# Attention stage of a hybrid block: GpSimd in written order, the reciprocals' read on its queue, the second head's loads up front, later loads by plan, both table loads ordered

## The chip, the cores and the metric

The kernel runs on one core of a Trainium2 chip. The metric is the device time of one launch in microseconds (us), the median of several runs. Before the change the runs took 1646.33, 1641.17 and 1647.93 us.

A core has five engines with a queue each: PE (TensorE, matmuls), DVE (VectorE), ACT (ScalarE), POOL (GpSimd) and SP (SyncE, here only for DMAs). Each works through its own instructions in order and waits on semaphores for the others. DMAs are issued by SP, ACT and POOL and run beside the engines.

## The reference, cut to what matters

One layer for 1024 tokens of width 1024: a modulated norm, a projection, two mixers side by side (causal attention with forget gates and an RWKV-7 recurrence), gates, an output projection and a convolutional feed-forward part. The change touches the attention:

```python
def fox_attention(q, k, v, log_f):
    seq = q.shape[2]
    cum = jnp.cumsum(log_f, axis=-1)
    scale = FOX_HEAD_DIM ** -0.5
    outs = []
    for blk in range(seq // Q_BLOCK):
        q0 = blk * Q_BLOCK
        q1 = q0 + Q_BLOCK
        logits = jnp.einsum('bhqd,bhkd->bhqk', q[:, :, q0:q1], k[:, :, :q1]).astype(jnp.float32) * scale
        logits = logits + cum[:, :, q0:q1, None] - cum[:, :, None, :q1]
        causal = jnp.arange(q1)[None, :] <= (q0 + jnp.arange(Q_BLOCK))[:, None]
        logits = jnp.where(causal, logits, -jnp.inf)
        probs = jax.nn.softmax(logits, axis=-1).astype(v.dtype)
        outs.append(jnp.einsum('bhqk,bhkd->bhqd', probs, v[:, :, :q1]))
    return jnp.concatenate(outs, axis=2)
```

There are 8 heads of width 64, and `Q_BLOCK` is 128. The gates, `jax.nn.sigmoid(p_gate)`, are computed in the same stage of the kernel.

## The kernel before

**Stages.** Projections and the recurrence come first, then attention, then the gated merge and the feed-forward part. Numbers are kept as pairs of a rounded high part and a low rest (`hi`/`lo`, `th`/`tl`), so that each product takes several matmuls.

**A head.** Queries and keys of head `h` lie in DRAM (`d_st`), as four pieces; values lie in `d_v`. `load_head(h)` (L1093) issues three DMAs on POOL: `stA` (two pieces, 1 MB), `stB` (two pieces of 68 rows, 544 KB) and `vh` (values, 512 KB). Each tag has two buffers, so the load of head `h + 2` needs the end of head `h`. Head 0 has tiles of its own (`first`).

**A block.** Each head takes four blocks `I` of 256 query rows, in the order 3, 0, 2, 1, and head 7 in the order 0, 1, 3, 2. `s_chain` issues the logits `lg`: for 512 columns one matmul with `stA` and one with `stB`. `softmax` (L1148) adds the mask and takes the maximum on DVE, then exponentiates on ACT with the row sums beside it (`P`). `t_chain` transposes `P` on PE (`tp`), `halve` splits it on ACT and DVE, and `a_chain` multiplies it with the values (`ov`). `collect` (L1271) copies `ov` into the tile `o` on ACT and adds its other half on DVE. There is one tile `o` for two heads and half of the rows: `o01` belongs to heads 0 and 1 and the second half of the rows, `o00` to the first half, `o11` and `o10` to heads 2 and 3. There are two buffers for these tiles, so `o10` reuses the one of `o00`.

**The reciprocals.** The softmax's division is made at the end. When the sums of half a head are there, `spread` (L1194) copies their reciprocals from PSUM into `rt`, writes them to DRAM (`d_rs`) and reads them back, broadcast over 64 partitions, as `R`. Both DMAs are issued by ACT. After the second head of a pair, POOL multiplies `o` by `R` (two halves, L1290), casts the result to `fx[0]` (L1293) and subtracts for the rest `fx[1]` (two halves, L1296). These five instructions are called a group here. The end of a group frees the buffer of its `o`.

**What sets the order.** PE's order is written out everywhere. In the attention stage that of DVE and ACT is too. A planner (`Weave`) keeps a clock of its own; the chains say when they want to go on, and between their steps it fills PE with matmuls for the gates (`rk_ps`, turned into gates by ACT at L1325 and L1328). POOL's order is left to the scheduler of the framework, which moved the loads up as far as it could: the load of `stA3`, written in head 2's second block, is issued when its buffer comes free.

**ACT's tables.** ACT loads a table for exp and tanh with `preload_act_table_set("exp_and_others")` (L1340). Nothing ties that instruction to others, and it stands at the program's start, where the next load replaces it. In attention the load is put in again ahead of the first gate (L1325).

Of the kernel before, what the change touches and what calls it, by code (L numbers as in the profile page):

```python
# [9 lines left out]
F32 = mybir.dt.float32  # L10
F32R = mybir.dt.float32r
# [5 lines left out]
S = 1024  # L17
KT = 8
NH = 512
# [11 lines left out]
for _name, _k in (("c", 8), ("ln1_g", 8), ("b_mod", 48), ("ln2_g", 8), ("mu", 14), ("w0", 4), ("a0", 4),  # L31
                  ("k_k", 4), ("k_a", 4), ("r_k", 4), ("ln_w", 4), ("ln_b", 4), ("conv_b", 22), ("conv_w", 66)):
    VEC[_name] = (_n, _k)
    _n += _k
NVEC = _n
NOSYNC = mybir.DependencyInfo(mybir.DependencyClass.NoSync, mybir.DependencyReason.DATA)

CST = {}
# [97 lines left out]
def hybrid_block(ctx: ExitStack, tc: tile.TileContext, a, out):  # L136
# [63 lines left out]
    sig_c = nc.scalar.activation(sc, V("c", 0, 8), AF.Sigmoid)  # L200
    nc.vector.tensor_tensor(sc, sc, V("c", 0, 8), op=ALU.mult)

    def use_ln_exp(after=None):

        i = nc.scalar.preload_act_table_set("natural_log_exp_and_others")
        if after is not None:
            tc.add_manual_dep(i.ins, after.ins.name, NOSYNC)


    d_gate = dr.tile([16, 128, S], F32, name="d_gate")  # L210
# [125 lines left out]
    def gate_steps(w, i, pps, ptag, pool, tag):  # L336
        if weave.late == 1:
            yield from late_gate(w, i)
            return
        for hf in range(2):  # L340
            cs = slice(hf * NH, hf * NH + NH)
            ps = pps.tile([128, NH], F32, tag=ptag, name=f"gt{i}_{hf}")
            yield from gemm_steps(ps, w[0:2], u, cs)

            g = pool.tile([128, NH], F32, tag=tag, name=f"gs{i}_{hf}")
            if weave.late:
                nc.scalar.activation(g, ps, AF.Tanh, scale=0.5)
# [6 lines left out]
            stt(g, ps, 0.0, g, op0=ALU.min, op1=ALU.subtract)  # L354
            nc.scalar.activation(g, g, AF.Exp)
            nc.sync.dma_start(d_gate[i, :, cs], g)


# [1 line left out]
    with ExitStack() as es:  # L360
# [563 lines left out]
        def main(k, p, hf):  # L924
# [97 lines left out]
            nc.scalar.activation(rs, rs, AF.Exp, scale=-0.5)  # L1022
# [60 lines left out]
    heads = {}  # L1083

    def load_first():

        parts = [d_st[0, 0], d_st[0, 1], d_st[0, 2, 0:68, :], d_st[0, 3, 0:68, :], d_v[0].rearrange("p a x -> p (a x)")]
        tiles = [fxp.tile([128, S], F32R, tag=f"h{t}", name=f"first{t}") for t in (3, 7, 2, 6, 5)]
        for t, x in zip(tiles, parts):
            marks["head"] = nc.gpsimd.dma_start(t[0 : x.shape[0], :], x)  # L1090
        heads[0] = *tiles[0:4], tiles[4].rearrange("p (a x) -> p a x", x=128)

    def load_head(h):  # L1093
        A = at.tile([128, 2, S], F32R, tag="stA", name=f"stA{h}")
        nc.gpsimd.dma_start(A, d_st[h, 0:2, :, :].rearrange("k r s -> r k s"))
        B = at.tile([128, 2, S], F32R, tag="stB", name=f"stB{h}")
        nc.gpsimd.dma_start(B[0:68, :, :], d_st[h, 2:4, 0:68, :].rearrange("k r s -> r k s"))
        vh = at.tile([128, 8, 128], F32R, tag="vh", name=f"vh{h}")
        nc.gpsimd.dma_start(vh, d_v[h])
        heads[h] = A[:, 0, :], A[:, 1, :], B[:, 0, :], B[:, 1, :], vh  # L1100

    load_first()
    while len(weave.queue) > 12:
        weave.step()
    fx = [[fxp.tile([128, S], F32R, tag=f"h{4 * x + p}", name=f"fx{x}{p}") for p in range(4)] for x in range(2)]
    weave.finish()
    weave.late = 1

    with tc.manual_schedule(engines={mybir.EngineType.DVE, mybir.EngineType.Activation}):
# [12 lines left out]
        def s_chain():  # L1122

            yield 3500
            for k, (h, I) in enumerate(seq):
                if k % 4 == 1 and h < 7:
                    load_head(h + 1)
                qa, ka, qb, kb, _ = heads[h]
                for i in (2 * I, 2 * I + 1):
                    n = (i + 1) * 128  # L1130
                    qs = slice(i * 128, i * 128 + 128)
                    yield from slot(pl_free if i > 3 else ps_free)
                    if i > 3 or i % 2 == 0:
                        yield from slot(lg_free)
                        lgt = pl.tile([128, S], F32, tag="lg", name=f"lg{h}_{i}")

                    lg = lgt[:, i % 2 * NH :] if i < 4 else lgt
                    for c0 in range(0, n, NH):
                        c1 = min(n, c0 + NH)
                        mm(lg[:, c0:c1], qa[:, qs], ka[:, c0:c1], start=True, stop=False)  # L1140
                        mm(lg[:, c0:c1], qb[0:68, qs], kb[0:68, c0:c1], start=False, stop=True)
                    if i > 3:
                        weave.spawn(softmax(h, (i,), lgt), 351)
                    elif i % 2:
                        weave.spawn(softmax(h, (i - 1, i), lgt), 351)
                    yield 0

        def softmax(h, rows, lgt):  # L1148
# [15 lines left out]
                part.append((i, n, nm, lg))  # L1164
            yield t + 140 - weave.now
            for i, n, nm, lg in part:
                e = (at.tile([128, S], F32, tag="P", name=f"P{h}_{i}", bufs=4) if i > 3 else
                     at.tile([128, NH], F32, tag="Ps", name=f"P{h}_{i}", bufs=2))
                if (h, hf) not in sums:
                    sums[h, hf] = at.tile([128, 8], F32, tag="sums", name=f"sums{h}_{hf}", bufs=4), []  # L1170
                sm, done = sums[h, hf]
                total = nm[:, 1:2] if h == 7 else sm[:, i % 4 : i % 4 + 1]
                nc.scalar.activation(e[:, 0:n], lg[:, 0:n], AF.Exp, bias=nm[:, 0:1], accum_out=total)
# [19 lines left out]

        def spread(h, hf, tp):  # L1194
            p = h // 2
            rt = at.tile([4, 128], F32, tag="rt", name=f"rt{h}_{hf}", bufs=1)
            nc.scalar.copy(rt, tp[0:4, 384:512])
            t = weave.use("ACT", weave.now, 260)
            yield t + 300 - weave.now
            nc.scalar.dma_start(d_rs[h, hf * NH : hf * NH + NH].rearrange("(i k) -> i k", k=128), rt)  # L1200
            if h % 2 == 0:
                norms[p, hf] = at.tile([128, NH], F32, tag="R", name=f"R{p}{hf}", bufs=2)
            yield t + 3500 - weave.now
            nc.scalar.dma_start(norms[p, hf][h % 2 * 64 : h % 2 * 64 + 64, :],
                                d_rs[h : h + 1, hf * NH : hf * NH + NH].to_broadcast([64, NH]))
            landed.add((h, hf))

# [28 lines left out]
        def halve(h, I, jj, tp, w, last):  # L1236
# [11 lines left out]
            tp_free.append(t + 210)  # L1248
            av_queue.append((t + 210, h, I, jj, th, tl))

        def a_chain():

            for _ in range(8 * 10):
# [3 lines left out]
                yield t - weave.now  # L1257
                if jj == 0:
                    yield from slot(ov_free)
                vh = heads[h][4]  # L1260
                order = [(0, th), (1, th), (1, tl), (0, tl)] if jj == I else [(0, th), (0, tl), (1, th), (1, tl)]
                for x, (k, t) in enumerate(order):
                    o0 = 128 if (jj == I and k == 1) else 0
                    mm(ov_ps[:, o0:256], vh[:, 2 * jj + k, :], t[:, 256 * k : 256 * k + 256 - o0],
                       start=jj == 0 and x == 0, stop=jj == I and x == 3)
                th_free.append(weave.now + 260)
                if jj == I:
                    weave.spawn(collect(h, I), 260)
                yield 0

        def collect(h, I):  # L1271
            p, hf, oc = h // 2, I // 2, slice(I % 2 * 256, I % 2 * 256 + 256)
            rows = slice(h % 2 * 64, h % 2 * 64 + 64)
            if (p, hf) not in halves:
                halves[p, hf] = at.tile([128, NH], F32, tag="o", name=f"o{p}{hf}"), []
            o, got = halves[p, hf]
            nc.scalar.copy(o[rows, oc], ov_ps[rows, :])
            yield weave.use("ACT", weave.now, 270) + 140 - weave.now
# [58 lines left out]
            while pending or (weave.cur is begun and begun is not None):  # L1337
                yield 300

        nc.scalar.preload_act_table_set("exp_and_others")  # L1340
        weave.run([a_chain(), t_chain(), s_chain()])
        weave.late = 2
        weave.run([drain()])
# [25 lines left out]
    def br_open(x, n):  # L1369
        if (x, n) not in br_raw:  # L1370
            br_load(x, n)
        raw = br_raw[x, n]
        hi = br.tile([128, NH], F32R, tag="whi", name=f"hi_br{x}{n}")
        lo = br.tile([128, NH], F32R, tag="wlo", name=f"lo_br{x}{n}")
        nc.scalar.copy(hi, raw)
# [764 lines left out]
```

## Time and profile before

| What | Value |
|---|---|
| median of 3 runs | 1646.33 us |
| the profiled execution, time | 1646.9 us |
| the profiled execution, span on the core | 1645.1 us |
| mean granted clock of PE | 0.991 |
| DMA, mean over the span | 147 GB/s |
| stA, stB and vh loads on POOL's queue | 7 each |
| writes of reciprocals and reads of R on ACT's queue | 14 each |

The span runs from the first to the last instruction of the program on the core; the time of the execution is a little longer. Busy time of PE counts matmuls whose ends are modelled. "Idle before" an instruction, in square brackets, is followed by what ended it, as inferred from semaphores. In rows of POOL and of the queues, buffer numbers are left out of the names: `stA` can be any head's.

### The profile page before, as it was taken

Reading aid. Unit: us, or ns where it says so; the run is one execution under the profiler, and the core shown is the slowest. Engines: PE = TensorE matmul, PEld = TensorE weight load, DVE = VectorE, ACT = ScalarE, POOL = GpSimd, SP = SyncE. Lnnn points to the kernel's source line nnn. Section 1 sums busy time; section 2 is a strip of 40 time slices with the busy share of each in tenths; the row PEclk is TensorE's granted clock in tenths of the full one; section 3 lists DMA queues with packets and bytes.
Section 4 is the critical chain, followed back from the end, with each engine's and each line's share of the span. In section 5 each row is a group of like instructions: output and inputs, shape, how many; then the busy total and the mean of one; then the engine's idle time right before and its main releaser. Section 6 shows DMA issues by size and latency. Waiting matters only on the chain.

```text
span 1645.1 us, 25963 instructions
## 1 busy us (share of the span) xinstructions
PE 1614.0 (98%) x9756; PEld 1327.9 (81%) x9756; DVE 1197.2 (73%) x2334; ACT 808.4 (49%) x1473; POOL 139.7 (8%) x169
## 2 busy tenths in 40 slices
PE   7999999999999999999999999999999999999998
PEld 5777877887887778788888888888888888888886
DVE  6875887887876636777579346887777777786677
ACT  7663434443455546676524135644444444555455
POOL 0011101211111020222132000000000000000000
PEclk8999999999999999999999999999999999999999
DMA  9587644543343236543487310242332232675363
GB/s 346 185 314 228 166 129 122 136 121 91 111 119 89 89 107 179 135 136 106 148 322 259 135 65 27 83 135 96 104 114 96 96 109 97 223 256 160 122 211 109
DMA packets 123902, 241.72 MB, mean 147 GB/s; under 512 B 39816, under 2 KB 48320, under 8 KB 123776
## 3 DMA queue, kind: packets, MB, share of 16 engines
q1 hardware_dynamic: 114944, 220.94, 41.3%
q0 software_dynamic: 7600, 17.25, 3.8%
q10 hardware_dynamic: 1232, 1.86, 0.4%
q8 instruction: 77, 1.26, 0.3%
q14 instruction: 49, 0.40, 0.1%
HBM read 174.43 MB, written 65.56 MB: 146 GB/s over the span
## 4 chain that ended last, share of the span: by engine, by line
PE 88%; DVE 6%; ACT 3%; DMA 1%; issue 1%; POOL 0%; SPq 0%; DVEq 0%; ACTq 0%; POOLq 0%
PE X L144 14%; PE D L144 13%; PE Y L144 6%; PE gt L144 6%; PE ps_rkv L144 6%; PE wo L144 5%; PE br L144 5%; PE rk_ps L144 4%; PE qk L144 4%; PE W L144 3%; PE v L144 3%; PE ov L144 2%; PE lg L144 2%; PE tp L151 2%; PE low L144 1%; PE sp L144 1%
## 5 line engine op out<-in xcount | busy, mean ns | idle before, releaser
L144 PE MATMUL D<-op,op 128*128 128x512 f32 x924 | 209.8, 389 | 0.0
L144 PEld LDWEIGHTS D<-op,op 128*128 128x128 f32 x924 | 173.3, 188 | 36.3 <-DVE op L1403 0.3
L144 PE MATMUL X<-T_m,S 128*128 128x512 f32 x440 | 107.3, 390 | 0.1
L144 PEld LDWEIGHTS X<-T_m,S 128*128 128x128 f32 x440 | 82.4, 188 | 18.2 <-ACT T_m L1828 0.6
L1402 ACT CAST op<-g 128x512 fp32r<-128x512 f32 x77 | 47.8, 621 | 73.0 <-PE D L144 48.1
L1403 DVE TENSOR_TENSOR op<-g,op 128x512 fp32r<-128x512 f32 x77 | 53.0, 688 | 41.3 <-ACT op L1402 41.3
L1639 DVE SCALAR_TENSOR_TENSOR c<-ab,vec,c 128x512 f32<-128x512 f32 x88 | 65.9, 749 | 19.5 <-ACT c L1642 17.9
L1603 DVE TENSOR_TENSOR S<-ur,S 128x512 fp32r<-128x512 f32 x66 | 45.5, 691 | 35.6 <-ACT S L1599 35.5
L1246 DVE TENSOR_TENSOR tl<-tp,th 128x512 fp32r<-128x512 f32 (+1 forms) x80 | 49.9, 633 | 28.0 <-ACT th L1238 24.5
L270 DVE TENSOR_TENSOR lo_in<-raw_in,hi_in 128x512 fp32r<-128x512 f32 x84 | 57.9, 728 | 15.9 <-PE gt L144 7.7
L1599 ACT CAST S<-ur 128x512 fp32r<-128x512 f32 x66 | 41.0, 622 | 55.6 <-DVE ur L1592 30.6
L1603 DVE TENSOR_TENSOR A<-ur,A 128x512 fp32r<-128x512 f32 x64 | 44.0, 688 | 30.9 <-ACT A L1599 30.7
L266 ACT CAST hi_in<-raw_in 128x1024 fp32r<-128x1024 f32 x42 | 43.9, 1048 | 45.2 <-PE ps_rkv L144 28.0
L144 PE MATMUL Y<-T_h,A 128*128 128x512 f32 x264 | 63.5, 389 | 0.0
L795 DVE TENSOR_TENSOR t<-E,M 128x60 f32<-128x60 f32 (+24 forms) x248 | 54.8, 221 | 11.8 <-DMA M<-sm 5.7
L144 PE MATMUL Y<-T_h,S 128*128 128x512 f32 x264 | 63.3, 389 | 0.0
L799 DVE TENSOR_TENSOR E<-E,t 128x60 f32<-128x60 f32 (+24 forms) x248 | 57.9, 234 | 5.8
L144 PE MATMUL X<-B_b,A 128*128 128x512 f32 x252 | 60.8, 390 | 0.0
L144 PE MATMUL W<-B_f,A 128*128 128x512 f32 x252 | 60.6, 389 | 0.0
L1238 ACT CAST th<-tp 128x512 fp32r<-128x512 f32 (+1 forms) x80 | 42.4, 542 | 33.7 <-PE tp L151 31.3
L144 PEld LDWEIGHTS Y<-T_h,A 128*128 128x128 f32 x264 | 49.5, 188 | 10.4
L144 PEld LDWEIGHTS Y<-T_h,S 128*128 128x128 f32 x264 | 49.5, 188 | 10.3
(494 smaller groups left out, 4071.6 us busy)
## 6 DMA issues: line engine op xcount, KB each, us to landing
raw_in<-in_w_in SPq DMA_DIRECT2D x50, 512.0 KB
wm<-in_w_mod SPq DMA_DIRECT2D x48, 512.0 KB
ur<-in_w_up SPq DMA_DIRECT2D x44, 512.0 KB
g<-d_g SPq DMA_DIRECT2D x35, 512.0 KB
d_g<-gs SPq DMA_DIRECT2D x44, 256.0 KB
d_g<-c SPq DMA_DIRECT2D x33, 256.0 KB
d_st<-qh SPq DMA_DIRECT2D x64, 128.0 KB
d_gate<-gs SPq DMA_DIRECT2D x32, 256.0 KB
```

The lines of the kernel that those rows point to most:

```text
L144: weave.last = nc.tensor.matmul(o, lhsT, rhs, start=start, stop=stop, skip_group_check=more)
L266: i = nc.scalar.copy(hi, raw)
L270: nc.vector.tensor_tensor(lo[:, c : c + NH], raw[:, c : c + NH], f32(hi[:, c : c + NH]), op=ALU.subtract)
L795: i = tt(tv, E32[:, 0:J, s : s + 1].to_broadcast([128, J, W]), M32[:, s : s + 1, s + 1 : 32].to_broadcast([128, J, W]), op=ALU.mult)
L799: tt(E32[:, 0:J, s + 1 : 32], E32[:, 0:J, s + 1 : 32], tv, op=ALU.add)
L1238: nc.scalar.copy(th[:, 0:w], tp[:, 0:w])
L1246: tt(tl[:, 0:w], tp[:, 0:w], f32(th[:, 0:w]), op=ALU.subtract)
L1402: nc.scalar.copy(hi, src)
L1403: tt(lo, src, f32(hi), op=ALU.subtract)
L1599: nc.scalar.copy(hi, src)
L1603: tt(lo, src, f32(hi), op=ALU.subtract)
L1639: stt(c, ab[:, x + hf * NH : x + hf * NH + NH], V("conv_w", 22 * x + i), c, op0=ALU.mult, op1=ALU.add)
```

## The change

- POOL's instructions stand in written order in the attention stage, as those of DVE and ACT do.
- The read of `R` is issued by POOL instead of ACT. `rt` has two buffers.
- Queries and keys of head 1 are loaded ahead of the stage. Those of heads 2 to 7 are issued at the second block of the head before, and each waits for the matmul that was last in the program there. Values are loaded on their own: for heads 1 and 2 at the third and fifth block, for later ones after the last `ov` of head `h`.
- `o` has three buffers. The four large `P` tiles of a head have the width that their rows need, one buffer for each.
- Both loads of ACT's tables name the activations that they come after: the last ones that need the table before.

```diff
+SYNC = mybir.DependencyInfo(mybir.DependencyClass.Sync, mybir.DependencyReason.DATA)
...
-    def use_ln_exp(after=None):
+    def use_ln_exp(*after):
         i = nc.scalar.preload_act_table_set("natural_log_exp_and_others")
-        if after is not None:
-            tc.add_manual_dep(i.ins, after.ins.name, NOSYNC)
+        for x in after:
+            tc.add_manual_dep(i.ins, x.ins.name, NOSYNC)
...
+    def fetch(dst, src):
+        i = nc.gpsimd.dma_start(dst, src)
+        tc.add_manual_dep(i.ins, weave.last.ins.name, SYNC)
+
+    def load_v(h):
+        values[h] = at.tile([128, 8, 128], F32R, tag="vh", name=f"vh{h}")
+        nc.gpsimd.dma_start(values[h], d_v[h])
+
+    def load_head(h, fetch):
         A = at.tile([128, 2, S], F32R, tag="stA", name=f"stA{h}")
-        nc.gpsimd.dma_start(A, d_st[h, 0:2, :, :].rearrange("k r s -> r k s"))
+        fetch(A, d_st[h, 0:2, :, :].rearrange("k r s -> r k s"))
         B = at.tile([128, 2, S], F32R, tag="stB", name=f"stB{h}")
-        nc.gpsimd.dma_start(B[0:68, :, :], d_st[h, 2:4, 0:68, :].rearrange("k r s -> r k s"))
-        vh = at.tile([128, 8, 128], F32R, tag="vh", name=f"vh{h}")
-        nc.gpsimd.dma_start(vh, d_v[h])
-        heads[h] = A[:, 0, :], A[:, 1, :], B[:, 0, :], B[:, 1, :], vh
+        fetch(B[0:68, :, :], d_st[h, 2:4, 0:68, :].rearrange("k r s -> r k s"))
+        heads[h] = A[:, 0, :], A[:, 1, :], B[:, 0, :], B[:, 1, :]
     load_first()
+    load_head(1, nc.gpsimd.dma_start)
...
-    with tc.manual_schedule(engines={mybir.EngineType.DVE, mybir.EngineType.Activation}):
+    with tc.manual_schedule(engines={mybir.EngineType.Pool, mybir.EngineType.DVE, mybir.EngineType.Activation}):
...
-                if k % 4 == 1 and h < 7:
-                    load_head(h + 1)
+                if k % 4 == 1 and 0 < h < 7:
+                    load_head(h + 1, fetch)
+                if k in (2, 4):
+                    load_v(k // 2)
...
-                e = (at.tile([128, S], F32, tag="P", name=f"P{h}_{i}", bufs=4) if i > 3 else
+                e = (at.tile([128, n], F32, tag=f"P{i}", name=f"P{h}_{i}", bufs=1) if i > 3 else
...
-            rt = at.tile([4, 128], F32, tag="rt", name=f"rt{h}_{hf}", bufs=1)
+            rt = at.tile([4, 128], F32, tag="rt", name=f"rt{h}_{hf}", bufs=2)
...
-            nc.scalar.dma_start(norms[p, hf][h % 2 * 64 : h % 2 * 64 + 64, :],
+            nc.gpsimd.dma_start(norms[p, hf][h % 2 * 64 : h % 2 * 64 + 64, :],
...
+                ends[h] = ends.get(h, 0) + 1
+                if ends[h] == 10 and 0 < h < 6:
+                    load_v(h + 2)
...
-                halves[p, hf] = at.tile([128, NH], F32, tag="o", name=f"o{p}{hf}"), []
+                halves[p, hf] = at.tile([128, NH], F32, tag="o", name=f"o{p}{hf}", bufs=3), []
...
-        nc.scalar.preload_act_table_set("exp_and_others")
+        table = nc.scalar.preload_act_table_set("exp_and_others")
+        for x in ("early", "rs"):
+            tc.add_manual_dep(table.ins, marks[x].ins.name, NOSYNC)
...
-    use_ln_exp(marks["gate"])
+    use_ln_exp(marks["gate"], marks["hi"])
```

The order of PE's and DVE's instructions does not change. On POOL, before, from the loads of head 3 to those of head 4 (a name's last digits are a running number; `R01_7206` is filled by two reads, one for each head of a pair, and `x2` is two equal rows):

```order
L1095 DMA stA3_7452<-d_st_95 128x2x1024
L1097 DMA stB3_7454<-d_st_95 68x2x1024
L1290 TENSOR_TENSOR o01_7118<-o01_7118,R01_7206 128x256 x2
L1099 DMA vh3_7456<-d_v_96 128x1024
L1293 CAST fx00_6889<-o01_7118 128x512
L1296 TENSOR_TENSOR fx10_6893<-o01_7118,fx00_6889 128x256 x2
L1290 TENSOR_TENSOR o00_7160<-o00_7160,R00_7277 128x256 x2
L1293 CAST fx00_6889<-o00_7160 128x512
L1095 DMA stA4_7726<-d_st_95 128x2x1024
L1097 DMA stB4_7728<-d_st_95 68x2x1024
L1296 TENSOR_TENSOR fx10_6893<-o00_7160,fx00_6889 128x256 x2
```

The same stretch of POOL in the changed kernel:

```order
L1096 DMA stA3_7452<-d_st_95 128x2x1024
L1096 DMA stB3_7454<-d_st_95 68x2x1024
L1215 DMA R01_7206<-d_rs_97 64x512
L1306 TENSOR_TENSOR o01_7118<-o01_7118,R01_7206 128x256 x2
L1309 CAST fx00_6893<-o01_7118 128x512
L1312 TENSOR_TENSOR fx10_6897<-o01_7118,fx00_6893 128x256 x2
L1101 DMA vh3_7547<-d_v_96 128x1024
L1215 DMA R00_7277<-d_rs_97 64x512
L1306 TENSOR_TENSOR o00_7162<-o00_7162,R00_7277 128x256 x2
L1309 CAST fx00_6893<-o00_7162 128x512
L1312 TENSOR_TENSOR fx10_6897<-o00_7162,fx00_6893 128x256 x2
L1096 DMA stA4_7726<-d_st_95 128x2x1024
```

The two reads of R have come in, each behind a load, and the loads of head 4 now stand behind both groups instead of inside the second one. The same stretch comes again for the loads of heads 5 and 6, with `o11`, `vh5` and `o10`.

ACT before, from the last gate ahead of attention to the first one inside it (`gs` are gates, `hi_in36` the high part of a gate's weights, `P0_6` the first probabilities):

```order
L277 CAST hi_in36_6929<-raw_in36_6927 128x1024
L351 ACTIVATE gs8_1_6915<-gt8_1_6842 128x512
L352 ACTIVATE gs8_1_6915<-gs8_1_6915 128x512
L353 ACTIVATE gs8_1_6915<-gs8_1_6915 128x512
L355 ACTIVATE gs8_1_6915<-gs8_1_6915 128x512
L1173 ACTIVATE P0_6_6979,sums0_1_6980<-lg0_6_6948,nm0_6_6960 128x896
L1325 ACT_TABLE_LOAD
L1325 ACTIVATE gs9_0_6982<-rk_ps_6925 128x512
```

ACT in the changed kernel, behind the same gate:

```order
L356 ACTIVATE gs8_1_6919<-gs8_1_6919 128x512
L1356 ACT_TABLE_LOAD
L278 CAST hi_in36_6933<-raw_in36_6931 128x1024
L1184 ACTIVATE P0_6_6977,sums0_1_6978<-lg0_6_6952,nm0_6_6964 128x896
L1341 ACTIVATE gs9_0_6980<-rk_ps_6929 128x512
```

The table load has moved from behind the first probabilities to behind the last older gate, and the cast of the weights now follows it. The load at the program's start is gone.

More of the change, by code (lines that the diff above doesn't have):

```diff
@@ L354, in gate_steps @@
             stt(g, ps, 0.0, g, op0=ALU.min, op1=ALU.subtract)
-            nc.scalar.activation(g, g, AF.Exp)
+            marks["early"] = nc.scalar.activation(g, g, AF.Exp)
             nc.sync.dma_start(d_gate[i, :, cs], g)
@@ L1021, in main @@
             nc.scalar.activation(rs, va, AF.Ln, scale=1.0 / CH, bias=epsr[:, 1:2])
-            nc.scalar.activation(rs, rs, AF.Exp, scale=-0.5)
+            marks["rs"] = nc.scalar.activation(rs, rs, AF.Exp, scale=-0.5)
             stt(y, y, V("ln_w", p), rs, op0=ALU.mult, op1=ALU.mult)
@@ L1082, in hybrid_block @@
     pt = es.enter_context(tc.tile_pool(name="pt", bufs=2, space=PS))
-    heads = {}
+    heads, values = {}, {}
     def load_first():
@@ L1090, in load_first @@
             marks["head"] = nc.gpsimd.dma_start(t[0 : x.shape[0], :], x)
-        heads[0] = *tiles[0:4], tiles[4].rearrange("p (a x) -> p a x", x=128)
-    def load_head(h):
+        heads[0] = tiles[0:4]
+        values[0] = tiles[4].rearrange("p (a x) -> p a x", x=128)
+    def fetch(dst, src):
[5 more added lines that the diff above has]
+    def load_head(h, fetch):
         A = at.tile([128, 2, S], F32R, tag="stA", name=f"stA{h}")
-        nc.gpsimd.dma_start(A, d_st[h, 0:2, :, :].rearrange("k r s -> r k s"))
+        fetch(A, d_st[h, 0:2, :, :].rearrange("k r s -> r k s"))
         B = at.tile([128, 2, S], F32R, tag="stB", name=f"stB{h}")
-        nc.gpsimd.dma_start(B[0:68, :, :], d_st[h, 2:4, 0:68, :].rearrange("k r s -> r k s"))
-        vh = at.tile([128, 8, 128], F32R, tag="vh", name=f"vh{h}")
-        nc.gpsimd.dma_start(vh, d_v[h])
-        heads[h] = A[:, 0, :], A[:, 1, :], B[:, 0, :], B[:, 1, :], vh
+        fetch(B[0:68, :, :], d_st[h, 2:4, 0:68, :].rearrange("k r s -> r k s"))
+        heads[h] = A[:, 0, :], A[:, 1, :], B[:, 0, :], B[:, 1, :]
     load_first()
+    load_head(1, nc.gpsimd.dma_start)
     while len(weave.queue) > 12:
@@ L1125, in s_chain @@
             for k, (h, I) in enumerate(seq):
-                if k % 4 == 1 and h < 7:
-                    load_head(h + 1)
-                qa, ka, qb, kb, _ = heads[h]
+                if k % 4 == 1 and 0 < h < 7:
+                    load_head(h + 1, fetch)
+                if k in (2, 4):
+                    load_v(k // 2)
+                qa, ka, qb, kb = heads[h]
                 for i in (2 * I, 2 * I + 1):
@@ L1249, in halve @@
             av_queue.append((t + 210, h, I, jj, th, tl))
+        ends = {}
         def a_chain():
@@ L1259, in a_chain @@
                     yield from slot(ov_free)
-                vh = heads[h][4]
+                vh = values[h]
                 order = [(0, th), (1, th), (1, tl), (0, tl)] if jj == I else [(0, th), (0, tl), (1, th), (1, tl)]
@@ L1374, in br_open @@
         lo = br.tile([128, NH], F32R, tag="wlo", name=f"lo_br{x}{n}")
-        nc.scalar.copy(hi, raw)
+        marks["hi"] = nc.scalar.copy(hi, raw)
         nc.gpsimd.tensor_tensor(lo, raw, f32(hi), op=ALU.subtract)
```

## The prediction

> **What bounds the kernel now.** I read the page first, then PE's waits, then the windows and the timelines around the longest wait in attention.
>
> ```profile
> span 1645.1 us, 25963 instructions
> PE 1614.0 (98%) x9756; PEld 1327.9 (81%) x9756; DVE 1197.2 (73%) x2334; ACT 808.4 (49%) x1473; POOL 139.7 (8%) x169
> ```
>
> PE (TensorE) is busy 98% of the span. The change leaves PE's and DVE's order as it was, and no matmul is added or taken away. So it can only win what PE idles, and what PE's clock loses, in the attention stage, from about 612 to 812 us.
>
> ```profile
> PE lg L144 <- ACT P L1173: 3.9, 4, 3.1
> PE rk_ps L144 <- ACT gs L1325: 2.5, 4, 1.2
> PE qk L144 <- DVE v L383: 2.3, 1, 2.3
> ```
>
> The columns are total, number and longest. The first two rows are attention's: 6.4 us in eight waits, of which one takes 3.1 and one 1.2. No row names a DMA there. The third row is from an earlier stage; I need it for the clock:
>
> ```profile
> 213.00:217.50 4.50, 2.24 (x20) 1.28 (x19) 2.53 (x9) 0.60 (x1) 0.00 (x0) 1.00 0.65 158
> 217.50:221.00 3.50, 3.50 (x39) 2.86 (x34) 3.26 (x11) 0.59 (x1) 0.00 (x0) 0.51 0.70 266
> 624.00:628.00 4.00, 3.30 (x18) 2.81 (x19) 1.18 (x4) 3.71 (x10) 0.00 (x0) 1.00 1.46 251
> 682.00:685.40 3.40, 0.34 (x3) 0.01 (x1) 1.80 (x4) 2.14 (x7) 1.23 (x2) 0.96 0.93 310
> 685.40:692.00 6.60, 6.60 (x22) 5.73 (x23) 2.72 (x5) 1.67 (x5) 0.00 (x0) 0.50 0.60 134
> ```
>
> Columns: the stretch, then the busy time of PE, PEld, DVE, ACT and POOL, the granted clock, DMA share, GB/s. After the 3.06 us wait, PE worked 6.60 us at half clock, which cost another 3.3. After the wait of 2.3 us near 216, it worked 3.50 us at 0.51, which cost 1.7. After the 1.2 us wait the clock stayed at 1.00. So a wait of 1.2 is cheap here, and one of 2.3 costs about 4.
>
> **The stall at 682, which the third "o" buffer removes.**
>
> ```profile
> 683.26 0.36 ACT L1277 COPY o<-ov 64x256 f32<-64x256 f32 x1 [4.65 <-POOL fx L1296]
> 685.40 0.79 PE L144 MATMUL lg<-stA 128*128 128x512 f32 x1 [3.06 <-ACT P L1173]
> ...
> 677.53 1.43 POOL L1290 TENSOR_TENSOR o<-o,R 128x256 f32<-128x256 f32 x2 [2.71 <-DMA R<-d_rs]
> 679.03 0.61 POOL L1293 CAST fx<-o 128x512 fp32r<-128x512 f32 x1
> 679.58 0.76 POOL L1095 DMA_DIRECT2D stA<-d_st  x1
> 680.34 1.00 POOL L1097 DMA_DIRECT2D stB<-d_st  x1
> 681.36 1.87 POOL L1296 TENSOR_TENSOR fx<-o,fx 128x256 fp32r<-128x256 f32 x2
> ```
>
> The copy into o10 needed the buffer of o00, which GpSimd's last subtraction held until 683.23, since GpSimd had waited 2.71 us for R and then issued stA4 and stB4 (1.76) first. ACT stood still for 4.65 us with the next probabilities queued behind the copy, and PE ran dry at 685.40 - 3.06 = 682.34. With three buffers, o10 takes the one of o01 instead. PE resumed 2.14 us after ACT did (685.40 - 683.26), so there is no PE wait if o01's buffer is free by 682.34 - 2.14 = 680.2. That would be worth 3.06 + 3.3 = 6.4 us.
>
> **The table load.**
>
> ```profile
> 618.14 0.63 ACT L355 ACTIVATE gs<-gs 128x512 f32<-128x512 f32 x1 [0.76 <-DVE gs L354]
> 621.64 1.01 ACT L1173 ACTIVATE P<-lg,nm 128x896 f32<-128x896 f32 x1 [2.87 <-DVE nm L1162]
> 622.76 1.28 ACT L1325 ACT_TABLE_LOAD   x1
> 624.70 2.14 PE L144 MATMUL rk_ps<-u_hi,hi_in 128*128 128x512 f32 x8 [1.18 <-ACT gs L1325]
> ```
>
> The load of 1.28 us stands ahead of the first gate's activation, and PE waits 1.18 us for that one. The change puts it before the 2.87 us in which ACT waits for DVE. The cast that moves behind it lasts 1.05 (the same form as at 677.56 below): 618.77 + 1.28 + 1.05 = 621.1, ahead of 621.64. Worth 1.2. The exp table's load that now stands at the program's start saves nothing: ACT soon waits for x anyway.
>
> ```profile
> 677.56 1.05 ACT L277 CAST hi_in<-raw_in 128x1024 fp32r<-128x1024 f32 x1
> 0.74 1.28 ACT L1340 ACT_TABLE_LOAD   x1 [0.74 <-PEq L2129]
> 7.74 1.06 ACT L454 ACTIVATE u_lo<-xt 128x1024 fp32r<-128x1024 f32 x1 [1.62 <-DMA xt<-in_x]
> ```
>
> **What the new order on GpSimd adds.** The reads of the reciprocals (R) leave ACT's queue. They cost ACT's sequencer time there but held up no PE work, so I count that as nothing, like the second rt buffer and the P tiles of exact width, whose buffers come round after the same number of tiles. What matters is where the reads land: on GpSimd's queue, right behind a head's two loads, in front of instructions that wait for them.
>
> ```profile
> stB<-d_st POOLq DMA_DIRECT2D x1, 544.0 KB, 20.1
> vh<-d_v POOLq DMA_DIRECT2D x1, 512.0 KB, 21.3
> ...
> DMA to landing us min/median/max: 11.5/12.3/24.1
> DMA to landing us min/median/max: 4.2/5.1/24.4
> R<-d_rs ACTq DMA_DIRECT2D x14, 128.0 KB
> ```
>
> The first two rows are head 1's loads, issued at 613.93 and 614.93, so they landed at 634.0 and 636.2; the next two are all of stB and all of vh. A vh otherwise lands after 4.2 to 5.1 us; issued behind a stB it took 21.3 and landed 2.2 us after it. I take this as: a transfer on this queue lands behind the stB ahead of it. [...]
>
> R is a quarter of a vh: 0.55 to 2.2 us behind the load ahead of it, and I take 1.0, nearer the short end since R is small. The other terms are a stB, with 0.75 for stA's issue ahead of it, 12.25 to 13.05 (I take 12.65); vh 4.2 to 5.1 (4.6); and one group of multiply, cast and subtract on GpSimd, 3.56, from the start of a group to that of the load behind it:
>
> ```profile
> 723.03 1.43 POOL L1290 TENSOR_TENSOR o<-o,R 128x256 f32<-128x256 f32 x2
> 726.59 0.76 POOL L1095 DMA_DIRECT2D stA<-d_st  x1
> ...
> 662.56 0.40 PE L144 MATMUL lg<-stB 68*128 68x512 f32 x1
> 677.94 0.40 PE L144 MATMUL lg<-stB 68*128 68x512 f32 x1
> 706.08 0.39 PE L144 MATMUL lg<-stB 68*128 68x512 f32 x1
> 710.12 0.39 PE L144 MATMUL lg<-stB 68*128 68x512 f32 x1
> 747.02 0.40 PE L144 MATMUL lg<-stB 68*128 68x512 f32 x1
> ```
>
> These PE rows are the matmul that releases stA3, the first uses of stB3 and stB4, the matmul that releases stA5, and the first use of stB6. The plan now lets stA3 go when the matmul at 662.56 ends, at 662.96. stB3 lands at 675.6, 2.3 us before its use at 677.94: no wait. Behind it R01 lands at 676.6 and the group on o01 ends at 680.2, just at the limit found above, so I count the old stall as gone (0.9 us earlier or 1.6 later by the bounds). Next stand vh3 and then R00: 680.2 + 4.6 + 1.0 = 685.8. The group on o00 ends at 689.3, and only then can stA4 go; its planned release, the end of lg3_7, would be near 683.3. stB4 lands at 702.0. Its first use, at 706.08 before, comes 6.4 earlier: 699.7. **PE waits 2.3 us** (0.2 with all short ends, 6.0 with all long ones).
>
> The same happens once more. stA5 goes free at 710.51, and 12.65 + 1.0 + 3.56 + 4.6 + 1.0 + 3.56 + 12.65 = 39.0 us later stB6 lands, at 749.5, against 747.02: **2.5 us** (0.4 to 6.2). No pair of groups stands ahead of the loads of heads 5 and 7. Taking stA2 and stB2 out of the rush at 616 helps no PE wait, since none there was for a DMA.
>
> The clock for a wait of 2.3 to 2.5: nothing by the 1.2 us row, 1.7 by the 2.3 us row, which is nearer. But such waits may fall otherwise against whatever decides it, so I take it for one of the two, 1.7, with 0 and 3.4 as ends. [...]
>
> **Sum.** -3.06 - 3.3 - 1.2 + 2.3 + 2.5 + 1.7 = -1.1 us. The profiled execution took 1646.9: 1645.8. It lies 0.6 over the median of the runs, 1646.33, so the forecast for the median is **1645.2 us**: most of what the third buffer wins is given back by later loads.
>
> **Rivals.**
>
> 1. *The reads are not held behind the loads.* Then the group on o01 starts as before, at 670.70, all loads go as planned, and the gains stand alone: 1646.9 - 7.6 = 1639.3, or 1638.7 against the median. For it: R moves little, and on ACT's queue it held nothing up. Against it: the vh rows. Chance 0.2.
> 2. *The late loads become the bound.* With long ends the waits are 6.0 and 6.2, and each halves the clock as the 3.06 us one did (3.3): 12.2 + 6.6 - 7.6 = +11.2, 1657.5. The place is the logits' second matmul of heads 4 and 6. It starts to lose where the two waits with their clock exceed 7.6: at 1.7 of clock each, from 2.1 us a wait, or 38.6 us from stA5's release to stB6's landing. The forecast is near that point, so slower by any amount has 0.4; waits of over 4 us, 0.1.
> 3. *The change doesn't do what it says:* o01's group ends 1.6 us past the limit, so the stall stays at 1.6 and may keep its half clock; with the two new waits that is 1645.2 + 1.6 + 3.3 = 1650.1. Chance 0.07, most of it within 0.5%.
>
> **How the numbers follow.** Forecast with waits of 1 to 4 us each, 1641 to 1650: 0.63. Rival 1: 0.2, rival 2's far part 0.1, rival 3: 0.07. The range 1638.5 to 1651.5 holds about eight tenths: it leaves out part of rival 1 and the far part of rival 2. A measurement of this kernel tells about 0.5%, 8.2 us, from no change. Faster by more needs nearly all of rival 1 and some luck: 0.10. Slower by more: 0.08. Within: 0.82.
>
> **What would show it.** The ACT row of the o10 copy without an idle time near 4.65; clock 1.00 near 685; no table load behind the first P. On GpSimd a wait for R of about 6 us ahead of the group on o01, and stA4 and stA6 issued about 6 us after the matmul that releases them. PE rows lg<-stB with an idle time of 1 to 4 us released by a DMA, at heads 4 and 6. Wrong would be: no PE wait for stB (rival 1), waits over 4 us with the clock at 0.5 behind both (rival 2), or a PE wait for a vh or any other head's stB, which I expect nowhere.

## The result, and the profile after

The changed kernel takes **1656.06 us** (median of 6 runs, 1654.73 to 1658.62). The kernel before took 1643.08 beside it (6 runs, 1640.32 to 1647.93). The ratio is 1.0077, with a 95% interval of 1.0058 to 1.0096: slower by 13 us, where 1 us faster was forecast, and outside the range of 1638.5 to 1651.5. The profiled execution took 1657.59, which is 10.7 more than that of before (1646.9).

The page of the changed kernel, its span and busy times:

```profile
span 1655.7 us, 25963 instructions
PE 1617.1 (98%) x9756; PEld 1331.3 (80%) x9756; DVE 1197.7 (72%) x2334; ACT 807.5 (49%) x1472; POOL 146.2 (9%) x183
```

PE's busy time rose by 3.1 us for the same matmuls: part of them ran at half clock (windows below). PE's waits in the changed kernel, with total, number and longest:

```profile
PE lg L145 <- DMA stB<-d_st: 12.1, 2, 6.3
PE rk_ps L145 <- ACT gs L1341: 1.3, 3, 0.6
PE lg L145 <- ACT P L1184: 0.9, 3, 0.5
```

The two rows of before have shrunk as forecast, from 3.9 to 0.9 and from 2.5 to 1.3. A row that before did not have is larger than both: 12.1 us in two waits for a stB.

ACT's timeline in the changed kernel, at the places that the prediction speaks of:

```profile
618.05 1.28 ACT L1356 ACT_TABLE_LOAD   x1
677.31 0.37 ACT L1293 COPY o<-ov 64x256 f32<-64x256 f32 x1 [0.94 <-DVE nm L1173]
```

The copy of o10 no longer waits for a buffer (4.65 before; 0.94 now, for a maximum from DVE), and the table load stands ahead of the first probabilities. PE's timeline at the two long waits:

```profile
703.75 0.80 PE L145 MATMUL lg<-stB 68*128 68x512 f32 x1 [6.27 <-DMA stB<-d_st]
752.82 0.80 PE L145 MATMUL lg<-stB 68*128 68x512 f32 x1 [5.81 <-DMA stB<-d_st]
```

They are at heads 4 and 6, where the prediction put them, but 6.27 and 5.81 long instead of 2.3 and 2.5.

Windows over the two stretches of half clock in the changed kernel (columns as in the prediction):

```profile
701.57:708.40 6.83, 4.65 (x14) 3.87 (x14) 2.59 (x5) 1.71 (x5) 0.00 (x0) 0.50 0.13 41
749.36:759.60 10.24, 6.78 (x20) 5.63 (x21) 4.09 (x8) 2.69 (x8) 0.00 (x0) 0.50 0.15 51
```

The clock is halved while PE still waits and stays so afterwards. PE worked 4.65 and 6.78 us at half clock, so the clock cost 2.3 + 3.4 = 5.7 us.

GpSimd's timeline in the changed kernel, from the loads of head 3 to those of head 4 and from those of head 5 to those of head 6. Only the first row of each group and some of the loads are shown:

```profile
661.03 0.73 POOL L1096 DMA_DIRECT2D stA<-d_st  x1 [9.17 <-PE lg L145]
673.67 1.42 POOL L1306 TENSOR_TENSOR o<-o,R 128x256 f32<-128x256 f32 x2 [10.35 <-DVE sums L1195]
683.92 1.43 POOL L1306 TENSOR_TENSOR o<-o,R 128x256 f32<-128x256 f32 x2 [5.55 <-DMA R<-d_rs]
687.48 0.76 POOL L1096 DMA_DIRECT2D stA<-d_st  x1
688.23 1.02 POOL L1096 DMA_DIRECT2D stB<-d_st  x1
...
710.71 0.73 POOL L1096 DMA_DIRECT2D stA<-d_st  x1 [19.82 <-PE lg L145]
726.23 1.42 POOL L1306 TENSOR_TENSOR o<-o,R 128x256 f32<-128x256 f32 x2 [13.23 <-DVE lg L1166]
734.64 1.43 POOL L1306 TENSOR_TENSOR o<-o,R 128x256 f32<-128x256 f32 x2 [3.72 <-DMA R<-d_rs]
738.19 0.76 POOL L1096 DMA_DIRECT2D stA<-d_st  x1
738.95 1.02 POOL L1096 DMA_DIRECT2D stB<-d_st  x1
```

In each stretch the second group waits for R (5.55 and 3.72 us), and stA stands at the end of it. stB4 and stB6 land where PE's two waits end, 15.5 and 13.8 us after their issue. For stB3 and stB5 the tile's own view, cut to one load at a time, has the landing:

```profile
L1096 POOL DMA_DIRECT2D stB<-d_st x1: 1013/1013/1013, 661.8 to 661.8; - x1
DMA to landing us min/median/max: 11.4/11.4/11.4
...
L1096 POOL DMA_DIRECT2D stB<-d_st x1: 1017/1017/1017, 711.4 to 711.4; - x1
DMA to landing us min/median/max: 14.4/14.4/14.4
```

From these rows the prediction's chain can be set beside what happened (us):

| Step | Forecast | heads 3 and 4 | heads 5 and 6 |
|---|---|---|---|
| stA issued to stB landed | 12.65 | 12.1 | 15.1 |
| to the first group's start (R) | 1.0 | 0.5 | 0.4 |
| first group, then vh and R, to the second group's start | 9.16 | 10.25 | 8.41 |
| second group, to the issue of stA | 3.56 | 3.56 | 3.55 |
| stA issued to stB landed | 12.65 | 16.3 | 14.6 |
| sum | 39.0 | 42.7 | 42.1 |

The chain has the links that were forecast. Of the 3.7 and 3.1 us by which it is longer, the two stB give 3.1 in the first stretch and 4.4 in the second; the links between them are 0.6 longer in the first and 1.3 shorter in the second.

### The profile page after: what moved, and what is told of

It is laid out like the page before. It is cut to its first block, busy times and chain, and to the rows that moved or that the text cites. A ratio compares the mean times of both kernels' runs of the same rounds, so it can differ in the third digit from the quotient of the medians.

```text
span 1655.7 us, 25963 instructions
## 1 busy us (share of the span) xinstructions
PE 1617.1 (98%) x9756; PEld 1331.3 (80%) x9756; DVE 1197.7 (72%) x2334; ACT 807.5 (49%) x1472; POOL 146.2 (9%) x183
## 4 chain that ended last, share of the span: by engine, by line
PE 82%; DVE 6%; DMA 5%; ACT 3%; issue 2%; SPq 1%; POOL 1%; DVEq 0%; ACTq 0%; POOLq 0%
PE X L145 13%; PE D L145 13%; PE Y L145 6%; PE gt L145 6%; PE ps_rkv L145 5%; PE wo L145 5%; PE br L145 5%; PE rk_ps L145 4%; PE W L145 3%; PE v L145 3%; PE qk L145 2%; DMA stB<-d_st 2%; PE ov L145 2%; PE lg L145 1%; PE low L145 1%
## 5 line engine op out<-in xcount | busy, mean ns | idle before, releaser
L271 DVE TENSOR_TENSOR lo_in<-raw_in,hi_in 128x512 fp32r<-128x512 f32 x84 | 60.1, 755 | 16.3 <-PE gt L145 7.3
```

Of the source, the lines that this page charges most:

```text
L271: nc.vector.tensor_tensor(lo[:, c : c + NH], raw[:, c : c + NH], f32(hi[:, c : c + NH]), op=ALU.subtract)
```

## The experiments

Theory: the loads of heads 4 and 6 are late because the reads of R stand behind stB on GpSimd's queue, the groups stand behind the reads and the next loads behind the groups. It takes the late planned release as well, and a stB that needs 12 to 16 us. Rivals: the wait for the planned release alone; the third buffer or the table; contention of other transfers.

**The reads back on ACT.** One line of the changed kernel:

```diff
-            nc.gpsimd.dma_start(norms[p, hf][h % 2 * 64 : h % 2 * 64 + 64, :],
+            nc.scalar.dma_start(norms[p, hf][h % 2 * 64 : h % 2 * 64 + 64, :],
```

> The changed kernel with the reads of R issued by ACT again, all else as in the change. Theory 1, the reads behind the loads hold the groups and so the loads of heads 4 and 6: the groups on o01 and o11 start some 4 us or more earlier against the release of stA3 and stA5, stA4 and stA6 go when the plan releases them, PE waits for no stB (12.1 us in the changed kernel), and the time is about 7 us under before, near 1636 us. Rival 2, the planned release alone is too late: 12 us of waits for stB stay, near 1655 us. Rival 3, the place of the loads behind both groups does it without R: one to three us are left of each wait, 1640 to 1648 us.

Measured: 1644.48 us (10 runs), ratio to before 1.0017 (1.0005 to 1.0030). GpSimd's timeline in this kernel, the second group's first row and the load of head 4:

```profile
679.04 1.44 POOL L1306 TENSOR_TENSOR o<-o,R 128x256 f32<-128x256 f32 x2
684.78 0.76 POOL L1096 DMA_DIRECT2D stA<-d_st  x1 [2.11 <-PE lg L145]
```

No wait for a stB is left in PE's waits. The second group starts without a wait for R (5.55 in the changed kernel), and stA4 goes when the plan lets it. So the place of the reads is one necessary part. The time is a little over that of the kernel before, though, and not the 1636 that was expected: PE's waits in attention still come to 5.7 us (2.2 in the kernel with the faster stB, further down). The longest is now another one, and ACT's timeline shows why:

```profile
PE rk_ps L145 <- ACT gs L1341: 2.5, 3, 1.8
```

```profile
652.89 0.46 ACTq L1215 DMA_DIRECT2D R<-d_rs  x1
653.40 0.60 ACT L1341 ACTIVATE gs<-rk_ps 128x512 f32<-128x512 f32 x1 [1.05 <-DMA d_rs<-rt]
```

On ACT's queue a read holds the activations behind it until the reciprocals are written, here 1.05 us, and PE waits 1.8 us for the gate behind it. The prediction took the reads on ACT to hold up no PE work; in this order they do. In the kernel with buffers and table alone, further down, the reads are on ACT too, and none of PE's waits for a gate is over 0.6 us. One thing that differs there is what runs beside the write of the reciprocals. Here the write is issued at 647.49 and the read behind it can go at 652.89, 5.4 us later; the planned loads stA2 and stB2 went at 643.15 and 643.85 and run beside it. There the same write and read stand at 642.80 and 646.48, 3.7 us apart, and head 2's loads had gone at 612.38, in the rush at the stage's start. That these loads delay the write fits both rows; no run tests it.

**No planned release.** The reads stay on GpSimd; the loads of heads 2 to 7 wait for their buffers only:

```diff
-                    load_head(h + 1, fetch)
+                    load_head(h + 1, nc.gpsimd.dma_start)
```

> The changed kernel without the wait of the loads for the plan's matmul: each load goes when its buffer is free and GpSimd reaches it. Theory 1: stA4 and stA6 stand behind the same two groups. stA3 and stA5 go earlier (by 5 us, when the head before ends), so the groups move up with them by about as much, and the PE waits for stB shrink from 6.3 and 5.8 to some 1 to 3 us each; 1642 to 1650 us. Rival 2, the planned release alone is too late: no waits for stB at all, near 1636 us.

Measured: 1639.19 us (10 runs), ratio 0.9982 (0.9969 to 0.9995). PE's waits for a stB in this kernel, and from its timeline the one at head 4:

```profile
PE lg L145 <- DMA stB<-d_st: 2.2, 2, 1.3
```

```profile
702.15 0.50 PE L145 MATMUL lg<-stB 68*128 68x512 f32 x1 [0.89 <-DMA stB<-d_st]
```

The waits for a stB fall from 12.1 to 2.2 us, with 0.89 left at head 4 and none at head 6 (the 1.3 is at head 1, in the rush at the stage's start). The wait is smaller than the 1 to 3 us expected, and the time 3 us under the expected range. stA4 is issued 15.3 us before PE needs stB4 (685.97 and 702.15 - 0.89) and not 10.0 (687.48 and 697.48), so the chain is as long as before (42.9 us from the issue of stA3, at 659.23, to stB4's landing) but starts sooner against PE. So the plan is the other necessary part: with either part gone, nearly all of the wait for a stB is gone.

**The values' loads moved away from stB4 and stB6.** The loads of vh4 and vh6 are written where heads 3 and 5 have had five of their products:

```diff
...
-                if ends[h] == 10 and 0 < h < 6:
+                if ends[h] == 10 and h in (1, 3, 5):
                     load_v(h + 2)
+                if ends[h] == 5 and h in (3, 5):
+                    load_v(h + 1, fetch)
```

> Only the loads of vh4 and vh6 move: from just behind stA4/stB4 (and stA6/stB6) on the same queue to before them, by being issued after the fifth product of heads 3 and 5. Theory (part of the waits of 6.27 and 5.81 us comes from vh running beside stB, which made stB4 land 16.2 us after the start of stA4's issue and stB6 14.6, where stB3 took 12.1): stB4 and stB6 land 12.0 to 13.2 us after the start of stA's issue, the two PE waits fall to 2 to 4 us, and the time falls by 4 to 8 us against the changed kernel, to about 1648 to 1652. Rival (the slow landing has another cause, such as the transfers of weights): landing still 14.5 to 16.5, waits 5.5 to 6.5, time within 2 us of the changed kernel.

Measured: 1652.39 us (6 runs), ratio 1.0046 (1.0030 to 1.0062). PE's waits for a stB in this kernel, GpSimd's issue of vh4, and the landings of stB4 and stB6 from the tile's view:

```profile
PE lg L145 <- DMA stB<-d_st: 8.5, 2, 5.0
```

```profile
704.14 0.57 POOL L1096 DMA_DIRECT2D vh<-d_v  x1 [13.96 <-PE ov L145]
```

```profile
L1096 POOL DMA_DIRECT2D stB<-d_st x1: 1015/1015/1015, 688.1 to 688.1; - x1
DMA to landing us min/median/max: 13.4/13.4/13.4
...
L1096 POOL DMA_DIRECT2D stB<-d_st x1: 1015/1015/1015, 737.2 to 737.2; - x1
DMA to landing us min/median/max: 13.4/13.4/13.4
```

vh4 came to stand behind stB4's landing rather than before its issue, so it is out of the way, and stB4 lands 2.1 us sooner (15.5 to 13.4). stB6 gains only 0.4 (13.8 to 13.4). The time lies 8.3 us over the kernel before measured beside it, where the changed kernel lies 13.0 over its own, and PE's waits for a stB fall by 3.6 us. The result lies between the two expectations: the wait at head 4, 3.5 us, is within the 2 to 4 of the first, that at head 6, 5.0, is not, and both stB land later than the first had them. So contention with vh is a real part at head 4 and a small one at head 6, some 4 to 5 of the 13 us in all. Why both still take 13.4 was not settled. stB3 took 12.1 in this execution; no vh ran beside any of the three, but two reads of R now stand directly behind stB4 and stB6, and one behind stB3. No run tests whether the second read costs the difference.

**A faster stB.** A stB has 68 rows. The changed kernel with stB as two transfers:

```diff
-        fetch(B[0:68, :, :], d_st[h, 2:4, 0:68, :].rearrange("k r s -> r k s"))
+        for r in (slice(0, 64), slice(64, 68)):
+            fetch(B[r, :, :], d_st[h, 2:4, r, :].rearrange("k r s -> r k s"))
```

> The changed kernel with stB loaded as two DMAs, of 64 and of 4 rows, in place of one of 68. If the 68 rows are slow because they go over four of the sixteen DMA engines, the 64 rows land 6 to 8 us after the issue of stA instead of 12 to 16, R lands as much earlier, and PE waits for no stB: about 1636 us. If stB is slow for its size or its place on the queue, it lands as late as before and the time stays near 1655 us.

Measured: **1637.86 us** (7 runs), ratio 0.9972 (0.9960 to 0.9983). The tile's view in this kernel, cut to the two parts of stB3 and then to those of stB4:

```profile
L1096 POOL DMA_DIRECT2D stB<-d_st x2: 606/616/627, 660.2 to 660.8; - x2
DMA to landing us min/median/max: 7.7/7.8/8.0
...
L1096 POOL DMA_DIRECT2D stB<-d_st x2: 609/612/616, 682.7 to 683.3; - x2
DMA to landing us min/median/max: 10.5/10.7/10.9
```

stB3 lands in 8 instead of 11.4 us and stB4 in 11 instead of 15.5, with vh4 still beside it. From stA's issue the 64 rows take 8.4 and 11.7 us, more than the 6 to 8 expected. The chain has two stB in it, and none of PE's waits in attention is for a load any more:

```profile
PE rk_ps L145 <- ACT gs L1342: 1.3, 3, 0.6
PE lg L145 <- ACT P L1185: 0.9, 3, 0.5
```

Reads, plan and order are those of the changed kernel: they cost 13 us only together with the long transfer. While the end of stB3 runs in the changed kernel, with its stA landed and no other load beside it (668.00 to 670.70), the DMA share is 0.30 of 16 engines, which would be 4.8 of them; with stB3 as two transfers (665.20 to 667.70) it is 0.90, or 14.4 of them. The four engines of the expectation were a supposition: the share is a mean and names no engine, so how the rows are spread is not shown.

**Buffers and table alone.** The kernel before with the third `o` buffer, the second `rt` buffer, the exact `P` tiles and the table load ordered; reads, loads and GpSimd's order as before:

```diff
...
-                halves[p, hf] = at.tile([128, NH], F32, tag="o", name=f"o{p}{hf}"), []
+                halves[p, hf] = at.tile([128, NH], F32, tag="o", name=f"o{p}{hf}", bufs=3), []
...
-        nc.scalar.preload_act_table_set("exp_and_others")
+        table = nc.scalar.preload_act_table_set("exp_and_others")
+        for x in ("early", "rs"):
+            tc.add_manual_dep(table.ins, marks[x].ins.name, NOSYNC)
```

> The kernel before with the change's buffers (three o, two rt, the exact P tiles) and its order of the exp table's load, but GpSimd's order, the reads and the loads as before. By the prediction's terms the stall of 3.06 us goes with 3.3 of clock, and 1.2 at the table: 7.6 us under before, near 1635.5 us. Rival: another wait takes the stall's place (o10 for its new buffer, or the groups), and the time stays within 2 us of before.

Measured: 1640.86 us (10 runs) against 1642.88, ratio 0.9980 (0.9969 to 0.9991). The stall is gone (PE's longest wait for probabilities is 0.5 us), but the medians differ by 2.0 us, not by the 7.6 of the prediction's gains. The interval of the ratio is 1.5 to 5.1 us, so 7.6 is outside it.

**The kernel before, profiled again**, to see whether the stall is there each time.

> The kernel before, unchanged, for a second profiled execution. If the stall at 682 (PE 3.06 us, then 6.6 us at half clock) is there in every execution, the third buffer should have won its 6.4 us against the median too, where buffers and table alone won 2.0. If it is smaller or absent here, the profiled execution that the prediction rested on was one of the longer ones, and the gain term was too large for the median.

In this second execution (1642.29 us), PE's waits for probabilities, and a window over the ten microseconds behind the longest of them:

```profile
PE lg L144 <- ACT P L1173: 2.1, 4, 1.2
```

```profile
682.20:692.00 9.80, 9.80 (x64) 8.64 (x65) 6.99 (x15) 7.30 (x19) 0.59 (x1) 1.00 0.65 140
```

The stall is there, but PE loses 1.2 us instead of 3.1, and the clock stays at 1.00. ACT's copy of o10 waited 2.79 us for GpSimd instead of 4.65. Here the third buffer can win 1.2 and the table 1.2: 2.4 us, near the 2.0 between the medians and inside the interval.

**The changed kernel, profiled again.**

> The changed kernel, unchanged, for a second profiled execution. Theory: two PE waits for stB, at heads 4 and 6, of 4.5 to 7 us each, followed by half clock, as in the first profile. Rival: the waits vary by more than that between executions, so that sizes read from one profile say little.

PE's waits for a stB in this execution, which took 1655.33 us:

```profile
PE lg L145 <- DMA stB<-d_st: 13.5, 2, 6.9
```

13.5 us in two waits, against 12.1 in the first profile. Unlike the old stall, which fell to less than half, the new waits came back as long.

**The faster stB without the new order**, that is buffers and table alone, and stB as 64 and 4 rows.

> The kernel before with the third o buffer, the second rt buffer, the exact P tiles, both table loads ordered (as in the run with buffers and table alone) and stB as two transfers of 64 and 4 rows. Theory (once the stall at 682 is gone, no load is late with GpSimd's order left to the scheduler, so a faster stB has nothing to win): within 3 us of that run's 1640.9, no PE wait for stB in either. Rival (the shorter transfer frees GpSimd's and the weights' transfers and wins as it did in the changed kernel): 1637 or less.

Measured: 1640.50 us (10 runs), ratio 0.9983 (0.9973 to 0.9994), as without the split. A faster stB wins where the loads are late, and nothing where they are not.

**The reads on SP**, whose queue in attention holds a few weight loads and the gates' writes; in the changed kernel `nc.gpsimd.dma_start(norms...` becomes `nc.sync.dma_start(norms...`. **Beside it the faster stB again.**

> The changed kernel with the reads of R issued by SP, whose queue in attention holds only three gate-weight loads and the writes of the gates. Theory (the reads are late because they stand behind stB on GpSimd's queue; on ACT's queue they are early but hold ACT): R lands about 3 us after its issue, both groups follow each other by GpSimd's own time, stA4 is issued when lg3_7 is done, no PE wait for stB over 0.5 us and none of PE for ACT over 1.2 us: 1637.5 to 1641. Rival (SP's queue holds the reads as GpSimd's did, behind a write of gates that waits for its data): a wait for R of several us on GpSimd, stB late again, 1645 or more.

> The changed kernel with stB as two transfers of 64 and 4 rows, a second time, beside the reads on SP. Theory: the first measure holds, 1637 to 1640, no PE wait for stB, and no difference of more than 2 us to the reads on SP, since neither leaves a PE wait for a load. Rival: the first measure (1637.9) was a lucky one, and this lies at 1640 or above, like the kernel before with buffers and table alone.

Measured: the reads on SP 1641.16 us (10 runs), ratio 0.9988 (0.9975 to 1.0001); the faster stB 1638.57 (8 runs), ratio 0.9964 (0.9952 to 0.9975). With the reads on SP, GpSimd's issues of stA4 and vh4, stB4's landing, PE's waits for a stB and the window behind the wait:

```profile
679.02 0.76 POOL L1096 DMA_DIRECT2D stA<-d_st  x1 [3.40 <-PE lg L145]
684.58 0.57 POOL L1101 DMA_DIRECT2D vh<-d_v  x1 [3.79 <-PE ov L145]
```

```profile
L1096 POOL DMA_DIRECT2D stB<-d_st x1: 1002/1002/1002, 679.8 to 679.8; - x1
DMA to landing us min/median/max: 17.5/17.5/17.5
```

```profile
PE lg L145 <- DMA stB<-d_st: 2.2, 1, 2.2
```

```profile
697.30:704.10 6.80, 6.75 (x20) 5.63 (x21) 2.87 (x6) 2.49 (x8) 0.00 (x0) 0.50 0.02 7
```

stA4 goes by plan (GpSimd waits 3.40 us for PE, not the other way round), as with the reads on ACT, and ACT is not held. So the reads' place is confirmed a second way. Yet a wait of 2.2 us is left, against the expectation of at most 0.5, so neither theory held whole: stB4, issued on time, took 17.5 us with a weight load (issued by SP at 679.85) and vh4 beside it, and the clock's half cost 3.4 more. The faster stB kept its lead in both measures. It lies 2.6 us under the reads on SP, a little more than was expected. It has the lowest median of all versions, 5 to 6 us under the kernel before and some 18 under the change; the kernel without the planned release, 1639.19, is not clearly behind it, since the intervals of the two ratios overlap.

## Why the prediction was wrong

Its mechanism was right and its sizes were not. What happened is its second rival, the late loads as the bound, to which it gave 0.1 and 1657.5 us with waits of 6.0 and 6.2. Its waits are close to those measured. That its time is so near 1656.06 is partly luck: it starts from a median that was 3.3 too high and takes off gains that were some 5 too large, and the two errors nearly cancel. By the prediction's steps:

- *The stall at 682 and the table load: gains of 3.06, 3.3 and 1.2.* Right for the execution that it was read from; the changed kernel shows neither. But that execution was among the longer ones of before. A second one has a stall of 1.2 and no half clock, and buffers and table alone win 2.0 us at the median. As terms for the median the gains were some 5 us too large. The prediction set that execution only 0.6 over the median, because of the three runs shown; later medians of before are 1642.9 to 1644.7.
- *The reads land behind the loads.* Right. The tile's view for the first group's R in the changed kernel:

```profile
L1215 POOL DMA_DIRECT2D R<-d_rs x1: 560/560/560, 662.8 to 662.8; - x1
DMA to landing us min/median/max: 10.8/10.8/10.8
```

  It landed at 673.6, behind stB3 (661.8 + 11.4 = 673.2). With the reads on ACT or SP the loads of head 4 are issued on plan.
- *A stB takes 12.25 to 13.05 us from stA's issue.* **This is the step that failed.** In the two chains it took 12.1, 16.3, 15.1 and 14.6. The long end, 13.05, is 0.75 and the median, 12.3, of the seven loads in the row that the prediction shows, so that three of the seven took longer than its longest case. One of these is the load of the very head in question; the tile's view cut to stB4, and SP's timeline, both of before:

```profile
L1097 POOL DMA_DIRECT2D stB<-d_st x1: 999/999/999, 680.3 to 680.3; - x1
DMA to landing us min/median/max: 14.8/14.8/14.8
```

```profile
686.20 0.33 SPq L258 DMA_DIRECT2D raw_in<-in_w_in  x1
```

  In before, stB4 landed 14.8 us after its issue, 15.6 after stA's, with a weight load beside it. With that row the wait at head 4 comes out at 2.3 + 2.9 = 5.2 and not 2.3. The range was taken from the loads of heads 3, 5, 6 and 7 (12.0, 11.5, 11.5 and 12.3). None of these had a vh beside it for long, and only head 7's had a load of weights, half as large as the one beside stB4 (256 KB, SP at 752.60). The text never asked what would run beside each stB in the new order. That is vh4 and vh6, which now follow their stB, and beside stB5 a weight load, by SP's timeline of the changed kernel:

```profile
720.69 0.33 SPq L259 DMA_DIRECT2D raw_in<-in_w_in  x1
```
- *The clock: 1.7 us, for one of two waits.* It was halved behind both, at 2.3 + 3.4 = 5.7 us. The longer waits are not the whole of it: with the reads on SP a wait of 2.2 us cost 3.4 too. The price of 1.7 came from one row, the wait near 216, and that wait (2.1 to 2.5 us) has another price in other executions: nothing in the profile of the reads on SP, 3.4 in the second one of the faster stB.
- *Sum.* With the measured waits and clock it is -7.6 + 12.1 + 5.7 = +10.2, against +10.7 between the two profiled executions. Between the medians it is 13.0: the profiled execution of before lay 3.8 over its median, that of after 1.5 over its own. With gains of 2.4 and the wait that stB4's row gives, and all else as it was, the prediction's sum would have been -2.4 + 5.2 + 2.5 + 1.7 = +7.0.
- *Rival 1* (reads not held) did not happen. *Rival 3* (the old stall stays) did not either.
- *Chances.* "Waits of over 4 us" had 0.1, since both waits were taken to need long ends at once. They share a cause: in the profiles of before and of the change every stB that had a load of 512 KB (a vh or weights) beside it for long took 13.8 us or more, and every one that had not 12.3 or less. Its own stA is not counted, since each stB has one.

What stays open: why stB4 and stB6 still need 13.4 us once vh is out of their way, and whether it is head 2's planned loads that delay the reads on ACT.

## What to carry to other kernels

When a transfer's time goes into a chain twice, take its time from the row of that very transfer and ask what will run beside it in the new order; the range over quiet ones is not a bound (11.5 to 12.3 us in before, 15.5 for stB4 in the new order). A small read that an engine must wait for should not stand on a queue behind a large load which that engine also issues (behind stB3, R landed 10.8 us after its issue; the quickest R of the changed kernel took 2.8), unless the load lands well ahead of need; if it must, make the large load fast first. A stall that is read from one profiled execution (3.06 us here, 1.2 in the second) is worth a second profile before it becomes a gain.

## What was not expected of the hardware

- 68 rows in one transfer took 11.4 us to land, as 64 and 4 rows 7.7 to 8.0 (both stB3, behind a stA and with no vh beside). The DMA share at the end of the two was 0.30 and 0.90.
- The clock stood at half in stretches of 3.4, 6.8 or 10.2 us, and a longer wait did not mean a longer stretch: behind the wait of 6.27 us it was 6.83, behind that of 5.81 us 10.24. Waits of 1.2 us brought none. One of 2.2 us brought a stretch of 6.8 with the reads on SP. The wait near 216, 2.1 to 2.3 us long in these three profiles, brought a stretch of 3.4 in that of before, 6.8 in the second one with the faster stB, and none in the one with the reads on SP. So waits of 2.1 to 2.3 us are not always free, and one row does not tell their price.
- A stB of head 3 or later took 11.4 us (stB3 of the changed kernel, no load beside it) to 17.5 us (stB4 with the reads on SP, a weight load and a vh beside it).
